# Two loads move to ACT's DMA queue, the first weights go ahead of the rest of x, and a 32-byte tile is added

## The chip, the core and the metric

The kernel runs on one core of a Trainium2 chip. A time is the device time of one execution in microseconds (us). Three runs of the kernel before took 2254.39, 2256.43 and 2259.61 us; their median is 2256.43 us.

## The reference, cut to what matters

A small network for 256 tokens of width 1024. x passes two hybrid layers (three kinds of attention, gates, an output product) and a final norm, then a second model of depth two with adaptive norms, feed-forward layers, a Fourier mixing layer and a retention layer. Nearly all of the arithmetic is `x @ w` with float32 weights.

```python
def hybrid_layer(x, norm_g, w_in, w_br_a, w_br_b, w_br_c, w_out, cos, sin):
    h = rmsnorm(x, norm_g)
    proj = h @ w_in
    ...
    merged = (gates[:, :, 0] * (ya @ w_br_a) + gates[:, :, 1] * (yb @ w_br_b) + gates[:, :, 2] * (yc @ w_br_c))
    return x + merged @ w_out
```

## The kernel before, in words

**Weights.** All weights stream from DRAM through `Stream` (lines 331 to 422) as some 350 items of up to 128 x 2048 floats (1 MB). `fill` issues the loads on SP's queue into one of three `raw` buffers. `split_next` cuts a raw unit into a high part `wh` (ACT copy, line 388) and a rest `wl` (DVE subtraction, line 389), four buffers each. Each product is three matmuls (high by high, high by rest, rest by high): lines 489 to 491 with the weights as the stationary operand and the activations streaming through, lines 640 to 642 and 1732 to 1734 with the activations stationary and the weights streaming. A streaming operand has 512 columns where both lanes of the second model, or 512 output columns, go together, and 256 where one lane goes alone.

**The start.** x is held transposed in `xl` as 8 blocks of 128 x 256; `load_x(i)` loads blocks 2i and 2i+1 (256 KB). The first 16 columns of the table `small` hold the gain that `block_in` needs. SP issues, in this order: x0, small, two of the four parts of weight item 0 (256 KB each, p0 and p1), x1, the parts p2 and p3, x2, x3, the two parts of item 1, the rest of `small`, `ident`, item 2. The list `waiting` holds the loads that `fill` drops in after every second part. ACT's first instruction is a copy of `ones` into `mhalf`, which brings ACT's table load; the copied values are overwritten by a DVE memset of `mhalf` (line 483). DVE then clears a tile `TH`, and two warm-up matmuls (line 1259) run on it. ACT then works strictly in order: `block_in` of blocks 0 and 1 (line 610), the casts of p0 and p1, blocks 2 and 3 and the first square (line 616), the cast of the unit p2+p3, and so on; DVE follows with `xo` (line 611), `wl` (389) and the sum of squares `ssum` (620, shared with POOL). TensorE's first chunk is 48 matmuls; after 36 of them the column sums of `ssum` (`pss`, line 576) stand in its program, ahead of the last 12.

**Where the tiles lie.** Pools take SBUF one behind another, in steps of 32 bytes per partition. From the low end come `keep` (x, small, ident, ones, mhalf, mods, sc and a few small tiles), then the weight ring (`raw`, `wh`, `wl`), then the pools of the stages. In the built program `keep` ends at byte 30,720, so `raw` begins at 30,720, `wh` at 55,296, `wl` at 71,680 and `xh` at 88,064: all multiples of 256. From the high end (`side=OTHER_SIDE`, lines 732, 733, 1635) comes the pool of the second model with `hh` at 185,344 and `ho` at 201,728, multiples of 256 too; its place depends on its own size alone. Some low-end stages begin with an unused tile `skew`: in the merge stage it has 32 floats in layer 0 and 40 in layer 1 (line 1171), so that `mh` and `mo` begin 192 and 224 bytes past a multiple of 256, and in the last feed-forward layer it has 48 floats (line 1309), so that `h1`, `o1` (printed as `h` and `o`), `ah` and `ao` of that layer begin 192 bytes past one. The `ah` and `ao` of the two-lane feed-forward layers, and `xh` and `xo`, begin at multiples of 256.

Of the kernel before, what the change touches and what calls it, by code (L numbers as in the profile page):

```python
# [21 lines left out]
F32 = mybir.dt.float32  # L22
# [308 lines left out]
class Stream:  # L331
# [21 lines left out]
    def fill(self):  # L353
        while self.n_dma < len(self.items) and len(self.raw) < self.bufs:
            key, cols, ap, off = self.items[self.n_dma]
            t = self.pool.tile([128, RAW], F32, name="raw", tag="raw", bufs=self.bufs)
            parts = 4 if self.n_dma == 0 else 2 if self.n_dma == 1 else 1
            w = cols // parts
            for i in range(parts):
                self.nc.sync.dma_start(t[:, i * w:(i + 1) * w],  # L360
                                       bass.AP(tensor=ap.tensor, offset=ap.offset + off + i * w,
                                               ap=[[cols, 128], [1, w]]))
                if i % 2 and self.waiting:
                    self.waiting.pop(0)()
            self.raw[self.n_dma] = t
            self.n_dma += 1
# [79 lines left out]
def build(tc, aps, stage=99):  # L446
    nc = tc.nc
    pe, act, dve, pool = nc.tensor, nc.scalar, nc.vector, nc.gpsimd
    from contextlib import ExitStack
    ctx = ExitStack()  # L450
    with ctx:
        P = ctx.enter_context(tc.tile_pool(name="keep", bufs=1))
# [8 lines left out]
        xl = P.tile([128, KB, T], F32, name="xl")  # L461
        small = P.tile([128, N_SMALL], F32, name="small")
        ident = P.tile([128, 128], F32, name="ident")
        ones = P.tile([128, 32], F32, name="ones")
        dve.memset(ones, 1.0)
        mhalf = P.tile([128, 8], F32, name="mhalf")
        act.copy(mhalf, ones[:, 0:8])

        def load_x(i):
            nc.sync.dma_start(xl[:, 2 * i:2 * i + 2].rearrange("p k t -> p (k t)"),  # L470
                              aps["xt"][:, 2 * i * T:(2 * i + 2) * T])

        load_x(0)
        nc.sync.dma_start(small[:, 0:16], aps["small"][:, 0:16])
        waiting = [lambda: load_x(1), lambda: (load_x(2), load_x(3)),
                   lambda: (nc.sync.dma_start(small[:, 16:], aps["small"][:, 16:]),
                            nc.sync.dma_start(ident, aps["ident"]))]

# [1452 lines left out]
```

## Time and profile before

| | us |
|---|---|
| median of three runs | 2256.43 |
| the profiled execution | 2255.87 |
| its span, first to last instruction | 2254.1 |
| TensorE busy in the span | 2222.9 |
| TensorE busy in the first 20 us | 14.05 |

The profiled execution's own time is 1.77 us above its span and 0.56 us below the median of the runs. Busy times of engines overlap and do not add up to the span. A matmul's duration in the trace includes the time in which its results drain, so successive matmuls overlap; what a stream of them costs is the distance from one start to the next.

### The profile page before, as it was taken

Reading aid. Unit: us, or ns where it says so; the run is one execution under the profiler, and the core shown is the slowest. Engines: PE = TensorE matmul, PEld = TensorE weight load, DVE = VectorE, ACT = ScalarE, POOL = GpSimd, SP = SyncE. Lnnn points to the kernel's source line nnn. Section 1 sums busy time; section 2 is a strip of 40 time slices with the busy share of each in tenths; the row PEclk is TensorE's granted clock in tenths of the full one; section 3 lists DMA queues with packets and bytes.
Section 4 is the critical chain, followed back from the end, with each engine's and each line's share of the span. In section 5 each row is a group of like instructions: output and inputs, shape, how many; then the busy total and the mean of one; then the engine's idle time right before and its main releaser. Section 6 shows DMA issues by size and latency. Waiting matters only on the chain.

```text
span 2254.1 us, 31045 instructions
## 1 busy us (share of the span) xinstructions
PE 2222.9 (99%) x12590; PEld 1901.8 (84%) x12590; DVE 1438.8 (64%) x2196; ACT 932.8 (41%) x1485; POOL 176.2 (8%) x207
## 2 busy tenths in 40 slices
PE   8999999999999999999999999999999999999998
PEld 7787887878988888899888888888888888889998
DVE  6776667767567766556666657755555666666555
ACT  5555544556532233356322333532232533335444
POOL 2100011012200000112000002100001100001000
PEclk9999999999999999999999999999999999999999
DMA  6343565444345554312445445335344323434553
GB/s 239 134 148 131 187 219 205 170 161 173 136 178 175 189 181 151 127 57 94 168 168 178 168 139 185 116 127 182 131 144 143 134 108 140 140 140 163 180 210 122
DMA packets 57167, 351.67 MB, mean 156 GB/s; under 512 B 6464, under 2 KB 6976, under 8 KB 23872
## 3 DMA queue, kind: packets, MB, share of 16 engines
q1 hardware_dynamic: 56016, 346.28, 43.5%
q10 hardware_dynamic: 1008, 3.41, 0.4%
q8 instruction: 98, 1.61, 0.3%
q14 instruction: 45, 0.37, 0.0%
HBM read 348.62 MB, written 1.05 MB: 155 GB/s over the span
## 4 chain that ended last, share of the span: by engine, by line
PE 85%; DVE 7%; ACT 4%; issue 2%; DMA 1%; POOL 0%; SPq 0%; DVEq 0%; POOLq 0%; ACTq 0%
PE pj L489 19%; PE pj L490 19%; PE pj L491 19%; PE pj L640 4%; PE pj L641 4%; PE pj L642 3%; DVE wl L389 3%; ACT wh L388 2%; PE pj L1732 1%; PE pj L1734 1%; PE pj L1733 1%; DMA raw<-w 1%; PE psc L950 1%; PE ada L527 1%; PE ppv L1078 1%
## 5 line engine op out<-in xcount | busy, mean ns | idle before, releaser
L389 DVE TENSOR_TENSOR wl<-raw,wh 128x1024 fp32r<-128x1024 f32 (+4 forms) x549 | 620.6, 1143 | 335.0 <-ACT wh L388 333.7
L388 ACT CAST wh<-raw 128x1024 fp32r<-128x1024 f32 (+4 forms) x549 | 521.9, 969 | 239.3 <-DMA raw<-w 144.6
L489 PE MATMUL pj<-hh,wh 128*128 128x512 f32 (+1 forms) x1216 | 448.5, 369 | 0.1
L490 PE MATMUL pj<-ho,wh 128*128 128x512 f32 (+1 forms) x1216 | 446.5, 367 | 0.8 <-POOL ho L727 0.5
L491 PE MATMUL pj<-hh,wl 128*128 128x512 f32 (+1 forms) x1216 | 446.0, 367 | 0.8 <-DVE wl L389 0.8
L516 DVE SCALAR_TENSOR_TENSOR acc<-raw,sc,acc 128x1024 f32<-128x1024 f32 x224 | 279.3, 1289 | 0.0
L489 PE MATMUL pj<-ah,wh 128*128 128x512 f32 (+1 forms) x770 | 267.9, 348 | 0.3 <-ACT wh L388 0.3
L491 PE MATMUL pj<-ah,wl 128*128 128x512 f32 (+1 forms) x770 | 266.2, 346 | 1.0 <-DVE wl L389 1.0
L489 PEld LDWEIGHTS pj<-hh,wh 128*128 128x128 f32 x1216 | 229.3, 189 | 44.5 <-ACT sg L1322 4.2
L490 PE MATMUL pj<-ao,wh 128*128 128x512 f32 (+1 forms) x770 | 265.8, 345 | 0.0
L491 PEld LDWEIGHTS pj<-hh,wl 128*128 128x128 f32 x1216 | 229.3, 189 | 38.9 <-DVE wl L389 1.0
L490 PEld LDWEIGHTS pj<-ho,wh 128*128 128x128 f32 x1216 | 229.3, 189 | 38.2 <-POOL ho L727 0.9
L640 PE MATMUL pj<-wh,xh 128*128 128x512 f32 (+2 forms) x480 | 191.8, 399 | 2.2 <-ACT wh L388 2.2
L641 PE MATMUL pj<-wl,xh 128*128 128x512 f32 (+2 forms) x480 | 185.1, 386 | 2.9 <-DVE wl L389 2.9
L642 PE MATMUL pj<-wh,xo 128*128 128x512 f32 (+2 forms) x480 | 184.5, 384 | 0.0
L1328 ACT CAST ah<-av 128x512 fp32r<-128x512 f32 (+1 forms) x84 | 47.5, 566 | 306.8 <-DVE av L1327 306.8
L489 PEld LDWEIGHTS pj<-ah,wh 128*128 128x128 f32 x770 | 145.0, 188 | 24.2 <-ACT wh L388 3.0
L491 PEld LDWEIGHTS pj<-ah,wl 128*128 128x128 f32 x770 | 145.0, 188 | 20.2 <-DVE wl L389 1.8
L490 PEld LDWEIGHTS pj<-ao,wh 128*128 128x128 f32 x770 | 145.1, 188 | 17.6
L670 POOL TENSOR_TENSOR ss<-ss,sq 128x256 f32<-128x256 f32 x55 | 44.9, 821 | 1284.3 <-ACT sq L668 1284.0
L1327 DVE TENSOR_TENSOR av<-sg,pj 128x512 f32<-128x512 f32 (+1 forms) x84 | 51.9, 618 | 131.7 <-PE pj L491 125.5
L1322 ACT ACTIVATE sg<-pj 128x512 f32<-128x512 f32 (+1 forms) x84 | 45.6, 543 | 176.9 <-PE pj L491 176.8
(344 smaller groups left out, 3591.9 us busy)
## 6 DMA issues: line engine op xcount, KB each, us to landing
raw<-w SPq DMA_DIRECT2D x258, 1024.0 KB, 4.8
raw<-w SPq DMA_DIRECT2D x64, 704.0 KB, 4.1
raw<-w SPq DMA_DIRECT2D x16, 768.0 KB, 4.2
de<-decay SPq DMA_DIRECT2D x24, 256.0 KB, 4.4
raw<-w SPq DMA_DIRECT2D x4, 904.0 KB, 4.5
raw<-w SPq DMA_DIRECT2D x6, 512.0 KB, 4.2
mk<-masks ACTq DMA_DIRECT2D x2, 768.0 KB, 6.0
xl<-xt SPq DMA_DIRECT2D x4, 256.0 KB, 6.3
```

What stands on the lines that cost most here:

```text
L388: self.nc.scalar.copy(hi[:, d], r[:, o])
L389: (sub or self.nc.vector).tensor_tensor(lo[:, d], r[:, o], hi[:, d].bitcast(F32), op=OP.subtract)
L489: pe.matmul(out, wh, xh, start=first, stop=False)
L490: pe.matmul(out, wh, xlo, start=False, stop=False)
L491: pe.matmul(out, wl, xh, start=False, stop=last)
L516: dve.scalar_tensor_tensor(acc[:, r, :], w, s, acc[:, r, :], op0=OP.mult, op1=OP.add)
L640: pe.matmul(o, xh[:, k, ts], wh[:, s], start=(k == 0), stop=False)
L641: pe.matmul(o, xh[:, k, ts], wl[:, s], start=False, stop=False)
L642: pe.matmul(o, xo[:, k, ts], wh[:, s], start=False, stop=(k == KB - 1))
L1322: act.activation(sg, pg[:, :N], AF.Silu)
L1327: dve.tensor_tensor(av, sg, pu[:, :N], op=OP.mult)
L1328: act.copy(ah[:, m, :], av)
```

## The change

`load_x(1)` and the first columns of `small` are issued on ACT's queue, ahead of ACT's first copy. SP issues x0, then all four parts of item 0, then x2 and x3; the rest follows as before. ACT's first copy writes a new tile `ap8` of 8 floats (32 bytes per partition) instead of `mhalf`, so the memset of `mhalf` no longer follows an ACT instruction. `ap8` is allocated in `keep` between `mhalf` and `mods`, so the low-end tiles allocated after it begin 32 bytes further on; the high-end tiles stay.

```diff
-                if i % 2 and self.waiting:
+                if (self.n_dma or i == 3) and i % 2 and self.waiting:
                     self.waiting.pop(0)()
...
         mhalf = P.tile([128, 8], F32, name="mhalf")
-        act.copy(mhalf, ones[:, 0:8])
 
         def load_x(i):
-            nc.sync.dma_start(xl[:, 2 * i:2 * i + 2].rearrange("p k t -> p (k t)"),
+            (nc.scalar if i == 1 else nc.sync).dma_start(xl[:, 2 * i:2 * i + 2].rearrange("p k t -> p (k t)"),
                               aps["xt"][:, 2 * i * T:(2 * i + 2) * T])
 
         load_x(0)
-        nc.sync.dma_start(small[:, 0:16], aps["small"][:, 0:16])
-        waiting = [lambda: load_x(1), lambda: (load_x(2), load_x(3)),
+        nc.scalar.dma_start(small[:, 0:16], aps["small"][:, 0:16])
+        load_x(1)
+        ap8 = P.tile([128, 8], F32, name="ap8")
+        act.copy(ap8, ones[:, 0:8])
+        waiting = [lambda: (load_x(2), load_x(3)),
                    lambda: (nc.sync.dma_start(small[:, 16:], aps["small"][:, 16:]),
                             nc.sync.dma_start(ident, aps["ident"]))]
```

## Rows read from the trace of the kernel before

**Rows 1.** The page, part 1: busy us, share of the span, instructions.
```profile
PE 2222.9 (99%) x12590; PEld 1901.8 (84%) x12590; DVE 1438.8 (64%) x2196; ACT 932.8 (41%) x1485; POOL 176.2 (8%) x207
```

**Rows 2.** Stretches: length, busy of PE, PEld, DVE, ACT, POOL; PEclk, DMA share, GB/s.
```profile
5.00:10.00 5.00, 4.36 (x15) 2.48 (x13) 2.91 (x6) 2.39 (x6) 0.00 (x0) 1.00 0.89 252
10.00:15.00 5.00, 2.65 (x7) 1.88 (x8) 3.42 (x5) 4.30 (x9) 1.84 (x2) 0.81 1.05 417
```

**Rows 3.** Chain of waits in the first 21 us: start, us, what.
```profile
2.59 0.43 SPq L470
...
3.54 6.88 DMA raw<-w
...
19.32 0.75 POOL ssum L620
```

**Rows 4.** Timeline of ACT: start, us, instruction [idle before <-releaser].
```profile
0.73 1.28 ACT L467 ACT_TABLE_LOAD   x1 [0.73 <-PEq L1923]
...
4.12 0.91 ACT L610 ACTIVATE xh<-xl,small 128x256 fp32r<-128x256 f32 x2 [1.90 <-DMA small<-small]
...
10.50 1.05 ACT L388 CAST wh<-raw 128x1024 fp32r<-128x1024 f32 x1 [1.42 <-DMA raw<-w]
...
13.17 1.05 ACT L388 CAST wh<-raw 128x1024 fp32r<-128x1024 f32 x1 [0.20 <-DMA raw<-w]
```

**Rows 5.** Timeline of the weight loads (PEld) at 20 us.
```profile
20.11 0.52 PEld L576 LDWEIGHTS pss<-ones,ssum 128*128 128x128 f32 x4 [0.54 <-POOL ssum L620]
```

**Rows 6.** Tiles xh, mh (layers 0, 1), h: ns min/median/max, first and last start.
```profile
L489 PE MATMUL pj<-xh,wh x32: 280/283/283, 46.2 to 57.4; 128*128 128x256 f32 x32
L489 PE MATMUL pj<-mh,wh x64: 276/276/364, 263.0 to 286.3; 128*128 128x256 f32 x64
L489 PE MATMUL pj<-mh,wh x64: 277/280/362, 549.9 to 573.6; 128*128 128x256 f32 x64
L489 PE MATMUL pj<-h,wh x352: 276/276/581, 2062.3 to 2214.5; 128*128 128x256 f32 x176
```

**Rows 7.** Timeline of PE, 256 columns: first and last of three even stretches.
```profile
270.71 0.28 PE L491 MATMUL pj<-mh,wl 128*128 128x256 f32 x1
...
272.98 0.28 PE L490 MATMUL pj<-mo,wh 128*128 128x256 f32 x1
...
555.00 0.28 PE L489 MATMUL pj<-mh,wh 128*128 128x256 f32 x1
...
559.62 0.28 PE L489 MATMUL pj<-mh,wh 128*128 128x256 f32 x1
...
578.47 0.28 PE L491 MATMUL pj<-hh,wl 128*128 128x256 f32 x1
...
580.27 0.28 PE L491 MATMUL pj<-hh,wl 128*128 128x256 f32 x1
```

**Rows 8.** Timeline of PE, 512 columns: first and last of two stretches.
```profile
23.42 0.39 PE L640 MATMUL pj<-wh,xh 128*128 128x512 f32 x1
...
25.92 0.39 PE L642 MATMUL pj<-wh,xo 128*128 128x512 f32 x1
...
29.77 0.40 PE L641 MATMUL pj<-wl,xh 128*128 128x512 f32 x1
...
32.08 0.39 PE L642 MATMUL pj<-wh,xo 128*128 128x512 f32 x1
```

**Rows 9.** Groups of PE by shape: count, busy us, mean ns, idle before.
```profile
L489 PE MATMUL pj<-hh,wh 128*128 128x512 f32 x960 | 375.6, 391 | 0.0
L489 PE MATMUL pj<-ah,wh 128*128 128x512 f32 x462 | 181.3, 392 | 0.0
L640 PE MATMUL pj<-wh,xh 128*128 128x512 f32 x384 | 157.1, 409 | 2.2 <-ACT wh L388 2.2
L489 PE MATMUL pj<-hh,wh 128*128 128x256 f32 x256 | 72.9, 285 | 0.1
L1732 PE MATMUL pj<-wh,hh 128*128 128x512 f32 x144 | 56.6, 393 | 0.0
```

## The prediction

> **What bounds the kernel now.** I read the page's busy shares first, then stretches, then the chain of waits of the start, and last the starts of single matmuls. TensorE is busy 2222.9 of 2254.1 us [rows 1], so two things can move the time: the few microseconds in which it stands still, most of them in the first 20 us, and the distance at which one matmul follows another.
>
> The start first. Between 5 and 15 us TensorE is busy 7.01 of 10 us [rows 2]. The chain of waits there runs through one transfer, the fourth part of the first weights (p3), issued at 3.54 and landed 6.88 us later [rows 3]; ACT stood idle 1.42 us for it and cast it at 10.50, and the next weights then came 0.20 us late at 13.17 [rows 4]. From there ACT, DVE and POOL follow without a gap that matters to the sum of squares, which ends at 20.07 [rows 3]; the column sums start at 20.11, and TensorE's weight loads had waited 0.54 us for it [rows 5]. So TensorE's own work of the start, slow clock included (granted 0.81 between 10 and 15 us, after its idle time [rows 2]), is nearly hidden: the start ends with p3's chain.
>
> Now the matmuls. Those of 256 columns, of one shape, have three speeds, and they go with the place of the streaming operand. xh, at a multiple of 256 bytes like the stationary weights, has a median of 283 ns; mh of layer 0 and h of the last feed-forward layer, 192 bytes past one, have 276; mh of layer 1, 224 past one, has 280 [rows 6]. From start to start that is, with 15 steps in 1.80 us, 120.0 ns for hh at a multiple of 256; with 20 steps in 2.27 us, 113.5 ns at 192; with 39 steps in 4.62 us, 118.5 ns at 224 [rows 7]. Matmuls of 512 columns all lie at multiples of 256. An undisturbed stretch takes 11 steps in 2.50 us, 227 ns; behind four transposes they need several matmuls to find back to that, and such a stretch takes 10 steps in 2.31 us, 231 ns [rows 8]. I read this so: the weights of the next matmul are loaded while the present one streams, both from SBUF, and what they cost each other depends on the distance of their addresses.
>
> The Trainium skill (TensorE: Matmul & The Clock Gate, Step-by-step: what each phase is for) says that "Loading the next tile's weights doesn't steal SBUF read bandwidth from the running matmul". By that rule addresses are free and the change is worth its start alone, 2256 us. The trace disagrees with the rule as far as 276 against 283 ns for one shape goes [rows 6]; for 512 columns no run here shows it yet.
>
> **The change part by part.** *The loads.* SP sheds two issues ahead of p3, small and x1; each costs 0.43 us and a gap of 0.04 [rows 3], so p3 is issued 0.94 us sooner. But x1 only changes its queue: ahead of p3's last byte stand x0, x1, p0, p1 and p2 as before, five times 256 KB, and the engines that move them are 0.89 busy at 252 GB/s [rows 2]. Bounds: all of the issue time is gained, -0.94 us, or the share that x1 now takes earlier from x0, p0 and p1 holds the in-order ACT up beyond its idle 1.42 us. x1 is 256 KB, 1.0 us at 252 GB/s; that fits into the 1.42, so +0.7 us is the far end, if two queues run less well than one. Nearest is "the same bytes": I take -0.2 us. x2, x3 and all later SP loads are issued 0.9 us sooner as well and stand behind the same bytes; POOL issues none.
>
> *ACT's two issues.* They stand ahead of its table load, and if they cost what SP's do, 2 x 0.43 us, the load of 1.28 us ends at 2.9 instead of 2.0 and the copy at 3.1. The first block of x was started at 4.12 after 1.90 us of idle time [rows 4], so 0.9 us are covered, with 1.0 left. Cost 0; without the cover 0.9 us, less ACT's later 1.42.
>
> *The memset of mhalf* no longer waits for ACT, so the warm-up matmuls come some 1.4 us sooner, and TensorE may stand idle between them and p0's weights. Should its first 12 matmuls run at the lower clock, twice 227 ns each, that is 2.7 us more; TensorE was idle for 10 - 7.01 = 3.0 us between 5 and 15 us [rows 2], most of it in wait for p3's weights, and the 0.54 us of waiting for the sum of squares [rows 5] takes up what is left. Cost 0, bound +0.5.
>
> *The tile ap8* moves the weight ring and every low-end stage by 32 bytes, and leaves hh and ho where they are. Pairs within the low end (xh, mh, h, ah with wh) keep their distance; pairs of hh or ho with wh or wl change theirs by 32 bytes. Their counts, three matmuls to a product: 256 columns, 256 x 3 = 768; 512 columns, (960 + 144) x 3 = 3312 [rows 9]. (Smaller groups of the same sort, some tenth of these, are left out.)
> For 256 columns hh would stand to its weights as mh of layer 1 does: 120.0 to 118.5, so 768 x -1.5 ns = -1.2 us; the ends are 0 and, at 113.5, -5.0.
> For 512 columns no row has this distance. Ends: the 113.5 of 256 columns, 6.5 ns less, and the disturbed stretch, 4 ns more. The 256s at 224 bytes lie between the two settled values, which I read as a stream that never settles, and an unsettled stream of 512 is the stretch at 231; part of its 4 ns is the transposes' own. I take +3 ns: 3312 x 3 = +9.9 us; ends -21.5 and +13.2.
>
> *Sum:* -0.2 + 0 + 0 - 1.2 + 9.9 = +8.5 us on the profiled execution's 2255.87, of which 2254.1 is its span: 2264.4. The median of the runs lies 0.56 above that execution; I say 2264.5, as both kernels scatter by more than that.
>
> **The rivals.** *The 512s hold 227.* They may find a settled distance of their own at any address. For it: they settle after each disturbance now [rows 8]. Against: at 224 bytes the 256s don't. Then -0.2 - 1.2, or -0.2 alone if addresses are free: 2254 to 2256.
>
> *Faster, on the other side.* The moved weights no longer meet the stream, as at 192 bytes. For it: every displaced case among the 256s is faster than the aligned one [rows 6]. Against: 32 bytes gave 1.5 ns where 64 gave 6.5. At half the far end, (-21.5 - 5.0) / 2 = -13 us: 2243. It decides from the point where hh's 512s start less than 226 ns apart.
>
> *The place alone counts,* not the distance. Then hh stays, and what moves pays: h, 352 x 3 from 113.5 to 118.5, +5.3 us; ah and the weights of line 640 with 512 columns, (462 + 384) x 3 x 3 ns = +7.6 [rows 6, 9]. For it: all stationary operands lie at multiples of 256 now, so the rows can't tell place from distance. Against: I see no partner for the stream but the weight load. 2255.87 - 0.2 + 12.9 = 2268.6, and more with the smaller groups.
>
> **How the numbers follow.** My forecast 0.44, the 512s hold 0.25, faster 0.17, place alone 0.14. A change under 0.2%, 4.5 us, can't be told from none here (the three runs of before span 5.2 us). Faster by more: 0.17 of the one rival and 0.02 of the second case's edge, 0.19. Slower: 0.44 + 0.14 less 0.06 where +3 ns proves to be under +1.7, 0.52. Within: 0.29. The forecast's own range is 2258 to 2270. The range of 8 in 10 takes in the held case and the place alone, and part of the faster one: 2248 to 2274.
>
> **What would show it.** Right: starts of hh's 512s some 230 ns apart and unsteady in long undisturbed stretches, hh's 256s at a median near 280 instead of 283, and xh, mh and h as in [rows 6]; the column sums still start between 19 and 20.6 us. Wrong: 227 or less for hh's 512s; mh of layer 0 at 280 and h at 280 (the place counts); or a wait of TensorE past 20 us that before did not have, as the moved weight buffers might be written more slowly, which no row here prices.

## The result and the profile after

The changed kernel takes 2278.46 us (median of 4 runs, 2273.64 to 2281.38), the kernel before beside it 2258.02 (2254.39 to 2260.89). The ratio is 1.0088, 95% interval 1.0069 to 1.0107: slower by 20 us. The profiled execution spans 2274.7 us, 20.6 more than before. The forecast was 2264.5 us, with 2248 to 2274 as the range of 8 in 10: the sign was right, the size was not.

First the page, part 1, of the kernel after (columns as in [rows 1]).

```profile
PE 2244.4 (99%) x12590; PEld 1900.5 (84%) x12590; DVE 1438.8 (63%) x2196; ACT 930.9 (41%) x1485; POOL 176.6 (8%) x207
```

The instructions are as many as before, and TensorE is busy 21.5 us longer. So the time is not in waits but in the matmuls themselves. Which ones, the groups by shape of the kernel after tell (all its lines from here on are numbered 2 higher than before; columns as in [rows 9]).

```profile
L491 PE MATMUL pj<-hh,wh 128*128 128x512 f32 x960 | 381.3, 397 | 0.0
L493 PE MATMUL pj<-hh,wl 128*128 128x512 f32 x960 | 379.6, 395 | 0.0
L492 PE MATMUL pj<-ho,wh 128*128 128x512 f32 x960 | 379.6, 395 | 0.0
L491 PE MATMUL pj<-ah,wh 128*128 128x512 f32 x462 | 181.2, 392 | 0.0
L642 PE MATMUL pj<-wh,xh 128*128 128x512 f32 x384 | 156.2, 407 | 2.4 <-ACT wh L388 2.4
L491 PE MATMUL pj<-hh,wh 128*128 128x256 f32 x256 | 72.5, 283 | 0.0
L492 PE MATMUL pj<-ho,wh 128*128 128x256 f32 x256 | 72.2, 282 | 0.9 <-POOL ho L729 0.5 <-POOL ho L1612 0.4
L493 PE MATMUL pj<-hh,wl 128*128 128x256 f32 x256 | 72.0, 281 | 0.8 <-DVE wl L389 0.8
L1734 PE MATMUL pj<-wh,hh 128*128 128x512 f32 x144 | 57.8, 401 | 0.0
L1736 PE MATMUL pj<-wh,ho 128*128 128x512 f32 x144 | 57.6, 400 | 0.6 <-DVE ho L725 0.6
L1735 PE MATMUL pj<-wl,hh 128*128 128x512 f32 x144 | 57.6, 400 | 0.0
```

[Rows 9] had the first member of each product; the other members in the kernel before:

```profile
L490 PE MATMUL pj<-ho,wh 128*128 128x512 f32 x960 | 373.7, 389 | 0.0
L491 PE MATMUL pj<-hh,wl 128*128 128x512 f32 x960 | 373.5, 389 | 0.0
...
L490 PE MATMUL pj<-ho,wh 128*128 128x256 f32 x256 | 72.7, 284 | 0.8 <-POOL ho L727 0.5 <-POOL ho L1610 0.3
L491 PE MATMUL pj<-hh,wl 128*128 128x256 f32 x256 | 72.5, 283 | 0.8 <-DVE wl L389 0.8
...
L1734 PE MATMUL pj<-wh,ho 128*128 128x512 f32 x144 | 56.2, 390 | 0.7 <-DVE ho L723 0.7
L1733 PE MATMUL pj<-wl,hh 128*128 128x512 f32 x144 | 56.1, 390 | 0.0
```

hh's three groups of 512 columns went from 391, 389 and 389 ns each to 397, 395 and 395. ah and the weights over xh, which moved by 32 bytes together with their weights, stayed: 181.3 and 181.2, 157.1 and 156.2. hh's 256s fell by 0.4 to 0.5 us a group. The tiles of [rows 6], of the kernel after:

```profile
L491 PE MATMUL pj<-xh,wh x128: 278/283/387, 45.2 to 436.9; 128*128 128x256 f32 x128
L491 PE MATMUL pj<-mh,wh x128: 276/278/367, 261.9 to 572.3; 128*128 128x256 f32 x128
L491 PE MATMUL pj<-h,wh x352: 276/276/582, 2083.0 to 2235.2; 128*128 128x256 f32 x176
```

xh 283 and h 276 are the medians of before at new addresses; mh pools both layers here, 276 and 280 before, and lies between. What kept its distance from its weights kept its speed. Last, starts in a long undisturbed stretch of hh's 512s, first and last of 20 (19 steps), of the kernel after, then of the kernel before:

```profile
649.65 0.40 PE L491 MATMUL pj<-hh,wh 128*128 128x512 f32 x1
...
654.09 0.40 PE L492 MATMUL pj<-ho,wh 128*128 128x512 f32 x1
```

```profile
649.64 0.39 PE L491 MATMUL pj<-hh,wl 128*128 128x512 f32 x1
...
653.94 0.39 PE L489 MATMUL pj<-hh,wh 128*128 128x512 f32 x1
```

4.44 us over 19 is 233.7 ns; 4.30 over 19 is 226.3, each good to about 0.5 ns, as the starts are rounded to 0.01 us: some 7 ns slower. The slower pace is a steady one: one step of 235 ns and one of 231 or 232 in turn, all through the stretch, where before each step has 226 or 227. And it does not depend on what goes on beside it. Of hh's steps of 512 columns, those during which VectorE, ScalarE and GpSimd all stand idle (some 600 in each kernel) have a mean of 233.4 ns after and 226.7 before, those during which no DMA is under way (some 1250 in each) 233.3 and 227.0, and all together 233.3 and 227.0. So traffic of other engines or of DMAs to the moved buffers is not the cause.

The start did gain. In the kernel after, the cast that [rows 4] had at 10.50 behind 1.42 us of waiting for p3 starts at 9.46 and waits for nothing, the next weights' cast at 11.81 for 13.17, and the column sums' weights are loaded at 19.05 for 20.11 [rows 5]:

```profile
9.46 1.03 ACT L388 CAST wh<-raw 128x1024 fp32r<-128x1024 f32 x1
...
11.81 1.04 ACT L388 CAST wh<-raw 128x1024 fp32r<-128x1024 f32 x1
```

```profile
19.05 0.52 PEld L578 LDWEIGHTS pss<-ones,ssum 128*128 128x128 f32 x4 [1.32 <-POOL ssum L622]
```

That lead is kept: matmul for matmul TensorE is 1.04 us ahead of the kernel before at 24 us, and still at 64 us. Up to that point the start is worse than in the kernel before, not better. ACT's first cast, at 4.94 before, comes at 6.92 after a wait for p0, and TensorE stands idle 2.36 us for it; from 8.80 to 11.79 us its matmuls of 512 columns start 0.43 us apart, at the lower of its two clock levels (granted 0.85 in the mean of 5 to 10 us and 0.81 of 10 to 15, columns as in [rows 2]):

```profile
6.92 0.62 ACT L388 CAST wh<-raw 128x512 fp32r<-128x512 f32 x1 [1.50 <-DMA raw<-w]
...
7.59 0.50 PE L642 MATMUL pj<-wh,xh 128*128 128x512 f32 x1 [2.36 <-ACT wh L388]
```

```profile
5.00:10.00 5.00, 2.42 (x6) 1.57 (x6) 3.08 (x6) 3.23 (x8) 0.00 (x0) 0.85 1.00 353
```

### The profile page after: what moved, and what is told of

Its sections match the earlier page's. It is cut to its first block, busy times and chain, and to the rows that moved or that the text cites. A ratio compares the mean times of both kernels' runs of the same rounds, so it can differ in the third digit from the quotient of the medians.

```text
span 2274.7 us, 31045 instructions
## 1 busy us (share of the span) xinstructions
PE 2244.4 (99%) x12590; PEld 1900.5 (84%) x12590; DVE 1438.8 (63%) x2196; ACT 930.9 (41%) x1485; POOL 176.6 (8%) x207
## 4 chain that ended last, share of the span: by engine, by line
PE 85%; DVE 7%; ACT 4%; issue 2%; DMA 1%; POOL 0%; DVEq 0%; POOLq 0%; SPq 0%; ACTq 0%
PE pj L491 19%; PE pj L493 19%; PE pj L492 19%; PE pj L642 4%; PE pj L643 3%; PE pj L644 3%; DVE wl L389 3%; ACT wh L388 1%; PE pj L1735 1%; PE pj L1736 1%; PE pj L1734 1%; DMA raw<-w 1%; PE psc L952 1%; PE ada L529 1%; PE ppv L1080 1%
## 5 line engine op out<-in xcount | busy, mean ns | idle before, releaser
L491 PE MATMUL pj<-hh,wh 128*128 128x512 f32 (+1 forms) x1216 | 453.8, 373 | 0.0
L492 PE MATMUL pj<-ho,wh 128*128 128x512 f32 (+1 forms) x1216 | 451.8, 372 | 0.9 <-POOL ho L729 0.5
L493 PE MATMUL pj<-hh,wl 128*128 128x512 f32 (+1 forms) x1216 | 451.6, 371 | 0.8 <-DVE wl L389 0.8
```

Of the source, the lines that this page charges most:

```text
L491: pe.matmul(out, wh, xh, start=first, stop=False)
L492: pe.matmul(out, wh, xlo, start=False, stop=False)
L493: pe.matmul(out, wl, xh, start=False, stop=last)
```

## The experiments

"Distance" is how far the streaming operand lies past the stationary one of the next load, modulo 256 bytes per partition. Line numbers differ by a few from kernel to kernel.

**The two parts of the change, each alone.** e1 keeps the loads and moves no address:

```diff
-        ap8 = P.tile([128, 8], F32, name="ap8")
-        act.copy(ap8, ones[:, 0:8])
...
         sc = P.tile([128, KB, 32], F32, name="sc")
+        act.copy(sc[:, 0, 0:8], ones[:, 0:8])
```

> The loads of the change alone: x1 and small on ACT's queue, item 0 ahead of x2 and x3, but ACT's first copy writes 8 columns of sc, so no address moves. Theory (the distance of hh from its weights costs, the loads pay a little): the column sums start at about 19.05 us as in the changed kernel instead of 20.11, hh's 512s follow each other at 227 ns, and the time is 1.1 us under the kernel before: 2257 where that is 2258, ratio 0.9995, hard to tell from 1. Rival (the loads' new order, for instance a queue that lags all through the run, costs the 20 us): 2278, ratio 1.009.

Measured: 2256.89, ratio 0.9989 (0.9974 to 1.0003). e2 is the kernel before and 32 bytes:

```diff
         mhalf = P.tile([128, 8], F32, name="mhalf")
+        gap = P.tile([128, 8], F32, name="gap")
+        dve.memset(gap, 0.0)
```

> The kernel before with an unused tile of 32 bytes behind mhalf (set by one memset), and nothing else: the loads stay. Theory (distance): hh's 512s at 232 to 235 ns, and the time is the changed kernel's and the 1.1 us that its loads gain: 2258 + 20.4 + 1.1 = 2279.5, ratio 1.0095. Rival (the loads): 2258, ratio 1.000.

Measured: 2278.61, ratio 1.0083 (1.0064 to 1.0102), that of the whole change. Of e2, then of e1, the column sums' weight load (timeline) and hh's group:

```profile
21.01 0.52 PEld L578 LDWEIGHTS pss<-ones,ssum 128*128 128x128 f32 x4 [0.72 <-POOL ssum L622]
```

```profile
L491 PE MATMUL pj<-hh,wh 128*128 128x512 f32 x960 | 381.3, 397 | 0.0
```

```profile
18.87 0.52 PEld L577 LDWEIGHTS pss<-ones,ssum 128*128 128x128 f32 x4 [1.63 <-POOL ssum L621]
```

```profile
L490 PE MATMUL pj<-hh,wh 128*128 128x512 f32 x960 | 375.6, 391 | 0.0
```

The slowdown is the unused 32 bytes. The loads bring the column sums forward: at 20.11 and 21.01 us with the old order, at 19.05 and 18.87 with the new one, and between 18.67 and 19.23 in all twelve kernels of this document that have it. In whole executions a gain of 1 us can't be told from none: the interval of e1 reaches from 5.9 us faster to 0.7 slower.

**Distance or place.** e4 makes ap8 256 bytes, e11 keeps it at 32 and moves hh and ho along:

```diff
-        ap8 = P.tile([128, 8], F32, name="ap8")
+        ap8 = P.tile([128, 64], F32, name="ap8")
...
```

> The changed kernel with ap8 of 256 bytes, so all low-end tiles move by 256 and hh is again at a multiple of 256 from its weights. Theory (distance modulo 256): hh's 512s at 227 ns, 256s at 120, time 2257, ratio 0.9995. Rival (any move of the low end against the high end costs, so the distance itself or the place counts): 512s at 232 to 235, time 2278.

```diff
-            Z["hh"] = bp.tile([128, KB, 512], F32R, name="hh")
-            Z["ho"] = bp.tile([128, KB, 512], F32R, name="ho")
+            for t in ("hh", "ho"):
+                v = bp.tile([128, KB * 512 + 64], F32R, name=t)[:, 8:8 + KB * 512]
+                Z[t] = v.rearrange("p (k t) -> p k t", k=KB)
```

> The changed kernel with its ap8, and hh and ho moved by 32 bytes as well: every address of the change stays, the distance is again 0. Theory (distance): 2257, hh's 512s at 227. Rival (weights at 32 past a multiple of 256 stream or load slower, whatever they meet): 2278.

Measured: e4 2258.0, ratio 0.9999 (0.9984 to 1.0013); e11 2255.27, ratio 0.9988 (0.9973 to 1.0003). hh's group in e4, then in e11:

```profile
L491 PE MATMUL pj<-hh,wh 128*128 128x512 f32 x960 | 375.6, 391 | 0.0
```

```profile
L491 PE MATMUL pj<-hh,wh 128*128 128x512 f32 x960 | 375.4, 391 | 0.0
```

In e11 every weight buffer lies where the change put it and the cost is gone. It is the distance, modulo 256 bytes; that 128 won't do in place of 256 is shown by e6 below.

**Other distances.** e3, e5, e6 and e7 widen ap8 to 64, 96, 128 and 160 bytes; e8 is e1 with hh and ho 16 bytes further on (as in e11, from column 4).

```diff
-        ap8 = P.tile([128, 8], F32, name="ap8")
+        ap8 = P.tile([128, 16], F32, name="ap8")   # in e5 24, in e6 32, in e7 40
...
```

> The changed kernel with ap8 of 64 bytes in place of 32, so hh lies 64 below a multiple of 256 past its weights (192). What the 256s show at that distance is 113.5 ns. Theory A (each distance has its own steady cost, and 512s follow the 256s: half of the cost at 0): hh's 256s at 113.5 ns, its 512s at 220; with 768 x -6.5 ns and some 3600 x -7 ns that is 2257 - 5 - 25 = 2227. Rival B (512s pay at any distance but 0, as at 32 bytes): 256s 113.5, 512s 233, 2257 - 5 + 23 = 2275. Rival C (what cost was that buffers began at an odd multiple of 32 bytes, not the distance): 512s 227, 2257.

> The changed kernel with ap8 of 96 bytes: hh streams past weights 96 bytes above a multiple of 256 from it (distance 160), and in the token projection the weights stream past hh at 96. Theory 1 (only multiples of 256 let 512s lock at 227; any other distance costs as 32 and 64 did): 512s at 230 to 234 ns, 2257 + 3617 x 3 to 6 ns = 2268 to 2279. Theory 2 (the cost falls with the distance from 0, and 32 and 64 are near to it): 227 or less, 2250 to 2257.

> The same with 128 bytes, half of the period, for both directions. Theory 1: 512s at 230 to 234 ns, 2268 to 2279. Theory 2: here the cost is lowest, 220 ns as the best distance of the 256s would give, 2257 - 25 = 2232.

> The same with 160 bytes: hh streams at distance 96 from its weights, the token projection at 160, the mirror of the run with 96. Theory 1 with a cost by distance alone: the two directions change places (hh's 512s show what the token projection's showed at 96, and the reverse). Rival (which operand is which decides): the projections keep their own values, different from those. Time 2257 + 3617 x the mean difference from 227.3 ns.

> The loads of the change without its moved addresses, and hh and ho shifted by 16 bytes inside tiles that are 256 bytes wider. In the kernel before, 452 columns at 16 bytes from their weights followed each other at 203.1 ns against 205.8 at 0. Theory A (512s do as those): 227.3 - 2.7 = 224.6 ns, 2257 - 3617 x 2.7 ns = 2247. Rival (16 bytes unsettle the 512s as 32 do): 233 ns, 2257 + 21 = 2278.

Measured: e3 2272.81, ratio 1.0064 (1.0041 to 1.0086); e5 2283.02, 1.0103 (1.0073 to 1.0134); e6 2273.05, 1.0059 (1.0037 to 1.0082); e7 2279.61, 1.0087 (1.0056 to 1.0117); e8 2270.34, 1.0051 (1.003 to 1.0072). hh with wh in e3, e5, e6, e7 and e8, in this order (391 before):

```profile
L491 PE MATMUL pj<-hh,wh 128*128 128x512 f32 x960 | 381.4, 397 | 0.0
```

```profile
L491 PE MATMUL pj<-hh,wh 128*128 128x512 f32 x960 | 382.2, 398 | 0.0
```

```profile
L491 PE MATMUL pj<-hh,wh 128*128 128x512 f32 x960 | 380.5, 396 | 0.0
```

```profile
L491 PE MATMUL pj<-hh,wh 128*128 128x512 f32 x960 | 378.5, 394 | 0.0
```

```profile
L490 PE MATMUL pj<-hh,wh 128*128 128x512 f32 x960 | 380.0, 396 | 0.0
```

These are one member of three, and the three share the cost unevenly. So the table has the mean from one start to the next over all 512-column matmuls that have another behind them, from the starts in the traces (gaps over 1.25 of the median left out), in ns. A first number is for hh over its weights (some 3050 matmuls), a second for weights over hh (some 570).

| distance | 0 | 16, 240 | 32, 224 | 64 | 96 | 128 | 160 | 192 |
|---|---|---|---|---|---|---|---|---|
| hh streams | 227.3 (before) | 231.7 (e8) | 233.3 (after) | | 233.4 (e7) | 232.6 (e6) | 234.2 (e5) | 233.3 (e3) |
| weights stream | in the same mean | 231.6 (e8) | 233.3 (after) | 230.0 (e3) | 233.4 (e5) | in the same mean | 234.1 (e7) | |

(At 0 the mean is over all 6370 such matmuls, hh's alone have 227.0; at 128 it is over both directions.) At every distance but 0 the 512s are slower, by 2.7 to 6.9 ns: theory 1 of e5 and e6, and half the period is no better than the rest. 96 and 160 give the same mean in either direction, so there the distance decides and not which operand is which. The hopes of e3 and e8 fell: at 192 hh's 512s do not follow the 256s down, and 16 bytes, which went with a faster pace for 452 columns, cost 4 ns here. hh's 256s missed their forecast in e3 as well: 116.3 ns from start to start where 113.5 was expected.

**Which weights the stream meets.** e9 displaces wl alone, e12 wh alone, by 32 bytes in the ring:

```diff
             hi = self.pool.tile([128, UNIT], F32R, name="wh", tag="wh", bufs=4)
+            if self.sp == 1:
+                self.nc.gpsimd.memset(self.pool.tile([128, 8], F32, name="gap", tag="gap", bufs=1), 0.0)
             lo = self.pool.tile([128, UNIT], F32R, name="wl", tag="wl", bufs=4)
+            if self.sp == 1:
+                self.nc.gpsimd.memset(self.pool.tile([128, 56], F32, name="end", tag="end", bufs=1), 0.0)
...
```

> The loads of the change without its moved addresses (a tile of 32 bytes stands in the ring between the buffers of wh and those of wl, and one of 224 behind them), so that wl alone lies 32 bytes past a multiple of 256 from all that streams. In a product of three matmuls (hh with wh, ho with wh, hh with wl) this tells which weights the stream meets. Theory (those loaded for the next matmul while it streams): the matmul of ho with wh, behind which wl is loaded, is followed some 6 ns later than 227, the two others at 227. Rival 1 (its own weights): the one of hh with wl is late. Rival 2 (the place of a whole group, no pair): all or none. About 2130 displaced matmuls of 512 columns, so 2257 + 13 = 2270 by the theory, if each pays as when all three are displaced.

(`sp` is 1 for the first unit only, so each tile is written once.) In e12 the first tile stands ahead of wh and the second ahead of wl. In both, ap8 is gone and ACT's first copy writes `sc`, as in e1.

> The counterpart of the run with wl displaced: the loads of the change, and wh alone 32 bytes past a multiple of 256 from all that streams (wl stays at 0). There the matmul of ho with wh, behind which wl is loaded, took 400 ns in the mean for 389, the one of hh with wl 389 as before, and the one of hh with wh 397 for 391, which the theory did not have. Theory 1 (a stream meets the weights loaded for the next matmul; the 6 ns were a disturbance handed on): hh with wl and hh with wh are late, ho with wh, behind which wl is loaded, takes 389. Theory 2 (it meets the load after next as well): ho with wh is late too, by some 6 ns, and hh with wl the most. Rival (its own weights): hh with wh and ho with wh are late, hh with wl is not. Time: some 4250 displaced matmuls of 512 columns at 6 ns or more, 2282 to 2295.

Measured: e9 2293.4, ratio 1.0154 (1.0131 to 1.0178; 2259.76 for the kernel before beside it); e12 2289.77, ratio 1.0133 (1.009 to 1.0176). The timeline of TensorE in e9 shows that each weight load starts with the matmul ahead of its own; behind it the three groups of e9, then those of e12:

```profile
612.03 0.40 PE L494 MATMUL pj<-hh,wh 128*128 128x512 f32 x1
612.03 0.19 PEld L495 LDWEIGHTS pj<-ho,wh 128*128 128x128 f32 x1
612.26 0.40 PE L495 MATMUL pj<-ho,wh 128*128 128x512 f32 x1
612.27 0.19 PEld L496 LDWEIGHTS pj<-hh,wl 128*128 128x128 f32 x1
```

```profile
L495 PE MATMUL pj<-ho,wh 128*128 128x512 f32 x960 | 383.7, 400 | 0.0
L494 PE MATMUL pj<-hh,wh 128*128 128x512 f32 x960 | 380.8, 397 | 0.0
L496 PE MATMUL pj<-hh,wl 128*128 128x512 f32 x960 | 373.7, 389 | 0.0
```

```profile
L494 PE MATMUL pj<-hh,wh 128*128 128x512 f32 x960 | 379.7, 395 | 0.0
L496 PE MATMUL pj<-hh,wl 128*128 128x512 f32 x960 | 379.0, 395 | 0.0
L495 PE MATMUL pj<-ho,wh 128*128 128x512 f32 x960 | 376.9, 393 | 0.0
```

In e9 the one matmul whose own weights were displaced, hh with wl, is the only one that kept its 389. ho with wh, under which wl is loaded, gained 11 ns. That is what the theory expects of these two, and not what rival 1 does. In e12 hh with wl, under which the displaced wh is loaded, gained the most, 6. But in e9 hh with wh gained 6 and in e12 ho with wh 4, with no displaced load under them. Theory 2 of e12 (the load after next counts too) fits which matmuls are late in both runs; that a late matmul hands something on is not excluded, though the one right behind the latest in e9 is unharmed. This stays open.

The size of e9 was missed once more, 2270 for 2293, because the 13 us priced the displaced loads alone. In e9 nearly all 6370 matmuls of 512 columns, not hh's only, belong to a product with one displaced load. From start to start they take 232.9 ns in the mean, 5.6 over before; 6370 times that is 35.7 us, and the profiled executions lie 35.5 apart. hh's own stand at 233.3 ns, as in the changed kernel, where all three loads of a product are displaced, and at 231.9 in e12, where two are. So here a product pays for one displaced load as much as for three, and e9 is slower than the change because more products are hit. None of the theories has that, and why it is so stays open too.

**A version meant to beat both.** e10 keeps the 512s at 0 and brings the 256s to 192:

```diff
...
-            hi = self.pool.tile([128, UNIT], F32R, name="wh", tag="wh", bufs=4)
-            lo = self.pool.tile([128, UNIT], F32R, name="wl", tag="wl", bufs=4)
+            z = skew(self.items[i][0])
+            both = self.pool.tile([128, 2 * UNIT + 64], F32R, name="wh", tag="wh", bufs=4)
+            hi, lo = both[:, z:z + UNIT], both[:, z + UNIT:z + 2 * UNIT]
...
```

(`skew` gives 16 floats where only 256s use the unit, 8 for the out projection of layer 1, and 0 elsewhere.)

> A version meant to beat both: the loads of the change, 512s left at multiples of 256, and the weights that only 256s use (the gate, first and last units of a two-lane feed-forward layer, the Fourier projection, the retention's q, the out projection of layer 1) written 64 bytes further on in their buffers (32 for the last), so their streams stand at 192. wh and wl of a unit share one wider tile, and sc is packed to make room. From 119.9 to 113.7 ns on 1740 matmuls and 118.3 to 113.7 on 192: 2257 - 10.8 - 0.9 = 2245, ratio 0.994 against the kernel before. If the 256s at 192 stand at 117.0 in a run instead of 113.7, as in two of the profiles, 2257 - 5 = 2252 at 192 for these alone. Rival (the gain at 192 belongs to those stages, not to the distance): 2257.

Measured: 2255.27, ratio 0.9979 (0.9965 to 0.9992): faster than the kernel before (2259.76 beside it) and than the change, but by 4.5 us where 14 were expected. And e11, without the skew, has the same 2255.27, so a gain of the skew itself is not shown. xh's 256s did speed up as expected, from 283 to 276 (e10):

```profile
L502 PE MATMUL pj<-xh,wh x128: 276/276/387, 45.3 to 434.6; 128*128 128x256 f32 x128
```

In the profiled executions the 256s of e10 take some 8 us less than e11's, from start to start, where 11.7 were forecast; and some 6 us more go into pauses and slower stretches (what a step takes beyond the median of its kind, for steps over 1.25 of it). The spans are 2248.8 and 2250.5 us. One place where the gain is given back is around the Fourier projection, 1000 to 1022 us, first e10, then e11 (stretches as in [rows 2]), and TensorE's waits of e10 there:

```profile
1000.00:1022.00 22.00, 20.91 (x168) 20.62 (x168) 11.36 (x18) 11.71 (x24) 4.37 (x6) 0.92 0.27 96
```

```profile
1000.00:1022.00 22.00, 21.65 (x182) 21.57 (x181) 11.35 (x19) 12.30 (x25) 5.12 (x7) 1.00 0.27 98
```

```profile
PE pss L691 <- ACT sq L681: 0.9, 1, 0.9
PE pss L690 <- DVE ss L683: 0.2, 1, 0.2
```

TensorE now arrives first and waits 1.1 us for sums of squares (0.3 in e11). After two microseconds, 1015 to 1017, in which it is busy less than half of the time, its granted clock falls to the lower level (0.50 from 1019 to 1021, 0.92 in the whole stretch). The matmuls were not what ended that stage.

## Why the prediction was right or wrong

**The cause** held: it is the distance, modulo 256 bytes, between the stream and the weights. Which load of a product counts how much stays open (e9 and e12). e2 has the whole slowdown, e1 has none of it, and e4 and e11 take it away by restoring the distance. "Place alone", "the 512s hold 227" and "faster" are refuted for 32 bytes.

**The failed step** is the term of hh's 512s, "I take +3 ns: 3312 x 3 = +9.9 us". It measured +5.7, +5.9 and +6.1 us on the three groups of 960, 17.7 in all or 6.1 ns each, and +4.1 on the three of 144 (168.9 to 173.0): 21.8 us, more than twice the term and over its upper end of 13.2. Two readings were wrong in it. I took the 231 of the stretch behind four transposes for a matmul stream out of step, so for the worst, and part of that for the transposes' own. But the displaced stream is not out of step: it runs steadily, 235 and 232 ns in turn. The 256s at 224 of [rows 7], from which the picture of a stream that never settles was taken, do go unevenly (39 steps of 115 to 123 ns in the trace); hh's 512s stand at 224 too and don't, so the sign came out right for a reason that did not hold. What sets the cost at a given distance stays open. And the bounds came from rows of other things, 256s at another distance and a disturbance at distance 0, so 4 ns was no bound. "Unsteady", under what would show the step right, was wrong with it.

**The 256s** measured -0.4, -0.5 and -0.5 us in three groups, -1.4 for the forecast -1.2, and their mean from start to start is 118.3 ns, that of mh of layer 1 at the same distance: here the reading by distance held in size too.

**The loads** brought the column sums 1.06 us forward where I took -0.2 with -0.94 as the far end. I had reasoned that p3 waits for the same bytes; its cast starts 1.04 us earlier and waits for nothing. That x2 and x3 now stand behind all of item 0, and the shorter queue of SP, are two reasons that no run separates. What the prediction feared of the start did come, p0's cast 1.98 us later and TensorE idle and then at its lower clock level, but it cost nothing at the end of the start: the column sums' weight load waited 1.32 us, so TensorE was early there all the same. ACT's two issues and the memset are in that too, and no run takes them apart.

Summed: 2255.87 - 1.06 - 1.4 + 21.8 = 2275.2, 1.3 under the profiled 2276.53, which the smaller groups, left out by the working, cover in part (pg: 18.7 to 19.0 us in each of three).

**The rule of the Trainium skill** that the prediction set aside (TensorE: Matmul & The Clock Gate, Step-by-step: what each phase is for: loading the next weights takes no read bandwidth from the running matmul) does not make addresses free here. The matmul of e9 under which the displaced wl is loaded takes 400 ns for 389, and neither its stream nor its own weights were moved. Whether it is read bandwidth that is lost, no run shows.

## What to carry to other kernels

A tile added anywhere below the weight buffers is a change of every matmul whose two operands lie on different sides of it. Pad such a tile to 256 bytes, or compare the addresses modulo 256 before and after. And where the nearest row is another shape or another disturbance, it is no bound: the range must reach past it, or leave the term open.

## What was not expected of the hardware

Of the distances tried none but 0 is good for 512 columns, while 256 columns run best at 192 (113.5 ns) and worse at 0 (120.0) [rows 7]; the two want different layouts, though e10, which gave each its own, shows no gain by it.

The pace of the 256s at 192 has two values at the same distance. The last feed-forward layer's h, median 276 in [rows 6], stood at 281 through the whole profiled execution of e1, and the span there was 2262.1 us against 2250.9 in e4:

```profile
L490 PE MATMUL pj<-h,wh x352: 281/281/582, 2063.5 to 2221.5; 128*128 128x256 f32 x176
```

That layer's 1580 matmuls of 256 columns (h, o, ah, ao) stand at 117.8 ns from start to start in e1 for 113.4 in e4, which is 7.0 of the 11.2 us; mh of layer 0, at 192 as well, keeps its 276 in e1. In e7 it is the other way round, h has 276 and mh of layer 0 has 281 (e7, 230 to 300 us):

```profile
L491 PE MATMUL pj<-mh,wh x64: 281/281/363, 262.1 to 285.5; 128*128 128x256 f32 x64
```

So the pace at 192 is not fixed for an execution but differs from stage to stage. The runs of the kernel before scatter from 2252.65 to 2265.31 us beside these kernels; such a switch may be a part of it, but no run shows that, and what sets the pace is open.
